# Seven products of quarters for the gate and up tiles, and issue in text order in the feed forward layers and the recurrence

## The chip, the core and the metric

The kernel runs on one core of a Trainium2 chip. Its engines are TensorE (PE in the profile, its weight loads PEld), VectorE (DVE), ScalarE (ACT), GpSimd (POOL) and SyncE (SP), which issues the DMAs. The metric is the device time of one execution in microseconds (us).

## The reference, cut to what matters

512 tokens of width 1024 go through two macaron layers (feed forward, mixer, feed forward; the mixer is stick-breaking attention in the first and a linear recurrence in the second) and then through two hybrid attention layers. All arrays are float32. The part that the change touches most is the feed forward layer, which occurs four times:

```
def sublayer_input(x, g, mod_j):
    shift, scale, gate = mod_j[:, 0], mod_j[:, 1], mod_j[:, 2]
    h = rmsnorm(x, g) * (1 + scale[:, None, :]) + shift[:, None, :]
    return h, (1 + gate)[:, None, :]

def swiglu(h, w_gu, w_down):                 # w_gu 1024 x 5632, w_down 2816 x 1024
    g, u = jnp.split(h @ w_gu, 2, axis=-1)
    return (jax.nn.silu(g) * u) @ w_down

mod = (silu(c) @ mod_w[layer] + mod_b[layer]).reshape(B, 3, 3, D_MODEL)
x = x + 0.5 * g * swiglu(h, ffn_w_gu[layer, 0], ffn_w_down[layer, 0])
```

The recurrence (`rglru_block`) projects h, convolves over four tokens, forms two sigmoid gates, runs a linear scan over the tokens, multiplies by gelu of a gate and projects back.

## The kernel before, in words

**Layout.** Everything is kept transposed: x, h and all projections are tiles of 128 features x 512 tokens. To reach float32 accuracy each operand is split into a rounded high part (fp32r, by a cast) and a low part (by a subtraction), and each product is three matmuls, high x high, high x low and low x high (`proj`). Matmuls accumulate in PSUM banks of 128 x 512; the tags are mm (four banks), z (two), T and o (one each).

**The weight stream.** All weights and modulation matrices are laid out on the host in the order of use (`segments`, `layout`) as entries of 128 x 1024. `stream_dma` loads entries into a ring of RAW = 4 buffers, `raw`. `stream_step` turns a weight entry into two chunks of 512 columns: the cast to `wh` on ScalarE, the subtraction to `wl` on VectorE, or on GpSimd for a share of them that `pool_low` sets (1.0 in `begin` and in the recurrence, 0 in the rest of the feed forward layers). A chunk holds four slots of 128 x 128, and `take` gives one slot to a row of matmuls, having run `stream_step` for AHEAD = 4 chunks in advance. A modulation entry is multiplied with silu(c) and summed on VectorE in one operation of 1024 columns (CUSTOM_DVE_ANT_0 in the profile) into one column of a modulation vector; the tuples at `mod(...)` in `segments` say between which fractions of a layer's entries the eight entries of each vector lie.

**A feed forward layer** (`ffn`) starts with the job "first": `begin` multiplies the weights of the first 4 columns (6 in the first layer) with x times the scale, before the norm's factor is known, while a chain (`factors`) sums the squares, takes the inverse root on VectorE, spreads it with TensorE and forms h in eight tiles `hH`, `hL`. The shift's share is added later by column sums `wshift` (`shift_cols`). Then 22 pairs f of a gate tile and an up tile follow, each tile 8 row blocks x 3 matmuls of 512 columns (jobs gu), with an evacuation `evac` on ScalarE and VectorE: silu, product, cast, low part. Last come 8 down tiles (jobs dn) of 22 x 3 matmuls each, after each of which x is updated, squared (GpSimd) and scaled for the next layer (`whole`).

**Order.** In the mixer attention and the hybrid layers a planner keeps one clock per engine (`clocked`) and a virtual time of TensorE, and all engines issue in the order of the program's text under `planned()`. In the feed forward layers and the recurrence the delays are fixed (`yield 0.7`) and, outside `begin`, the framework's own scheduler orders the instructions of an engine. In the recurrence (`lru`), `second` waits until all ten `om` tiles exist and then issues the ten scans (`beta`), after which the gelu outputs `ge` follow.

The planner's prices, in `clocked`, for n columns:

```
vector:  d = 0.15 + n / 960.0            clock advances by d - 0.082
         if not bank and n > 8: d += 0.58 * (overlap with GpSimd's operations)
scalar:  d = (0.162 if bank else 0.2) + n / 1210.0
gpsimd:  d = 0.12 + n / (440.0 if two else 900.0)      clock advances by d - 0.045
mm:      cost = max(0.112, 0.007 + n * 0.00043)
```

In the profile line L547 is the matmul in `mm`, L551 the transposition, L328 the helper that passes on every operation of VectorE, ScalarE and GpSimd.

## Time and profile before

| | |
|---|---|
| time, median of 3 runs | 3085.96 us (3082.9 to 3088.1) |
| the profiled execution | 3085.68 us, its span 3084.0 us |
| TensorE | 2977.1 us busy, 97%, 13752 matmuls |
| VectorE, ScalarE, GpSimd | 62%, 43%, 35% busy |
| DMA | 400.53 MB, mean 130 GB/s, 39.2% of the 16 engines |

The profile is one execution, with times from the start of its span. A matmul's recorded time overlaps that of its neighbours, so its price is the distance from one start to the next. A row of a group gives the busy time, the mean of one in ns, the idle time ahead of it on its engine, and what ended that.

### The profile page before, as it was taken

How to read it: one execution, taken by the hardware profiler on the slowest of the kernel's cores; microseconds unless marked ns; L12 is line 12 of the kernel's file. 1: busy time of each engine (PE TensorE's matmuls, PEld its weight loads, DVE VectorE, ACT ScalarE, POOL GpSimd, SP SyncE). 2: the span in 40 equal slices, each digit the busy share in tenths (PEclk: the TensorE clock that was granted, in tenths of full speed). 3: DMA queues.
4: the chain of work that ended last, by engine and by line, in shares of the span. 5: the costliest groups of instructions: out<-in, count | busy, mean ns of one | idle time of the engine just before them, and what ended most of it. 6: DMA issues, size and time to landing. Idle time of an engine off the chain costs nothing. (4 is left out here: it accounts for less than half of the span.)

```text
span 3084.0 us, 39072 instructions
## 1 busy us (share of the span) xinstructions
PE 2977.1 (97%) x13752; PEld 2475.4 (80%) x13752; DVE 1902.0 (62%) x3409; ACT 1312.9 (43%) x2520; POOL 1085.0 (35%) x802
## 2 busy tenths in 40 slices
PE   7999999989999999999899999999999999999998
PEld 5788877768888888887688888888888878888886
DVE  7844476676444655568965333578676556867653
ACT  3333245544332333324734333356456534645652
POOL 4554754440001200013531001343443684334466
PEclk9999999999999999999999999999999999999999
DMA  6454554413333344462222223354343335434322
GB/s 241 158 198 175 194 160 113 119 64 137 137 137 133 120 171 152 156 211 82 81 94 92 96 97 115 110 166 122 103 123 110 109 117 157 123 110 124 110 85 93
DMA packets 132643, 400.53 MB, mean 130 GB/s; under 512 B 18528, under 2 KB 19040, under 8 KB 132448
## 3 DMA queue, kind: packets, MB, share of 16 engines
q1 hardware_dynamic: 132448, 398.04, 39.2%
q8 instruction: 109, 1.79, 0.2%
q14 instruction: 86, 0.70, 0.1%
HBM read 343.44 MB, written 6.30 MB: 113 GB/s over the span
## 5 line engine op out<-in xcount | busy, mean ns | idle before, releaser
L328 POOL TENSOR_TENSOR wl<-raw,wh 128x512 fp32r<-128x512 f32 x574 | 815.3, 1427 | 905.1 <-ACT wh L328 852.2
L328 ACT CAST wh<-raw 128x512 fp32r<-128x512 f32 x968 | 596.0, 620 | 1063.3 <-PE mm L547 926.9
L547 PE MATMUL mm<-hH,wh 128*128 128x512 f32 x1584 | 622.1, 393 | 13.6 <-ACT ge L328 9.8
L547 PE MATMUL mm<-hL,wh 128*128 128x512 f32 x1584 | 620.6, 392 | 2.6 <-DVE hL L328 2.6
L547 PE MATMUL mm<-hH,wl 128*128 128x512 f32 x1584 | 619.7, 391 | 0.0
L328 DVE TENSOR_TENSOR wl<-raw,wh 128x512 fp32r<-128x512 f32 x396 | 290.3, 735 | 363.4 <-ACT wh L328 360.7
L547 PE MATMUL mm<-gH,wh 128*128 128x512 f32 x1016 | 407.2, 401 | 6.2 <-DVE v L328 3.9
L547 PE MATMUL mm<-gH,wl 128*128 128x512 f32 x1016 | 398.5, 392 | 1.5 <-POOL wl L328 1.5
L547 PE MATMUL mm<-gL,wh 128*128 128x512 f32 x1016 | 397.8, 392 | 0.0
L547 PEld LDWEIGHTS mm<-hH,wh 128*128 128x128 f32 x1584 | 299.6, 189 | 77.4 <-ACT ge L328 10.2
L547 PEld LDWEIGHTS mm<-hL,wh 128*128 128x128 f32 x1584 | 299.7, 189 | 67.0 <-DVE hL L328 5.3
L547 PEld LDWEIGHTS mm<-hH,wl 128*128 128x128 f32 x1584 | 299.5, 189 | 62.5
L328 DVE CUSTOM_DVE_ANT_0 raw<-raw,cact 128x1024 f32<-128x1024 f32 x144 | 207.8, 1446 | 187.0 <-DMA raw<-ws 180.1
L547 PE MATMUL mm<-aH,wl 128*128 128x512 f32 x704 | 274.0, 389 | 0.0
L547 PE MATMUL mm<-aH,wh 128*128 128x512 f32 x704 | 273.9, 389 | 0.0
L328 POOL TENSOR_TENSOR sq<-x 128x512 f32<-128x512 f32 x7 | 7.6, 1086 | 730.7 <-DVE x L328 730.7
L547 PEld LDWEIGHTS mm<-gH,wl 128*128 128x128 f32 x1016 | 191.4, 188 | 44.7 <-POOL wl L328 2.7
L547 PEld LDWEIGHTS mm<-gH,wh 128*128 128x128 f32 x1016 | 192.1, 189 | 42.0 <-issue 4.3
L547 PEld LDWEIGHTS mm<-gL,wh 128*128 128x128 f32 x1016 | 192.1, 189 | 35.0
L547 PEld LDWEIGHTS mm<-aH,wl 128*128 128x128 f32 x704 | 132.1, 188 | 27.6 <-POOL wl L328 0.4
L547 PEld LDWEIGHTS mm<-aH,wh 128*128 128x128 f32 x704 | 132.1, 188 | 27.5
L547 PE MATMUL mm<-wide,wh 128*128 128x512 f32 x384 | 149.4, 389 | 0.0
(271 smaller groups left out, 4706.6 us busy)
## 6 DMA issues: line engine op xcount, KB each, us to landing
raw<-ws SPq DMA_DIRECT2D x629, 512.0 KB, 3.3
ks<-rH SPq DMA_DIRECT2D x80, 128.0 KB, 3.2
kl<-rL SPq DMA_DIRECT2D x80, 128.0 KB, 2.6
qs<-rH SPq DMA_DIRECT2D x56, 128.0 KB, 3.9
qs<-rL SPq DMA_DIRECT2D x56, 128.0 KB, 3.7
keep<-ws SPq DMA_DIRECT2D x16, 256.0 KB, 5.9
ks<-qkH SPq DMA_DIRECT2D x32, 128.0 KB, 3.5
kl<-qkL SPq DMA_DIRECT2D x32, 128.0 KB, 3.1
```

What stands on the lines that cost most here:

```text
L328: r = f(*args, **kw)
L547: self.nc.tensor.matmul(out, lhsT, rhs, start=start, stop=stop, skip_group_check=True)
```

## The change

The gate and up tiles of 43 of the 88 pairs f are no longer computed as two tiles of eight row blocks, but as a 2 x 2 product of quarters in seven products (Strassen's scheme in Winograd's form): a, b are the gate's weights for the first and the second half of the 1024 features, c, d those of up, and the moving side is cut into two halves of 256 tokens. `SEVEN` names the pairs. Four sums of weights (s1 to s4) are formed by VectorE or GpSimd on the raw entries, then cast and split like other weights; `turned` forms the four sums of the moving side once per layer. Each product has 4 row blocks x 3 matmuls of 256 columns; the results are combined from PSUM by additions of 256 columns. The lookahead in these pairs is 6 chunks. The last product of a pair is run inside the next pair (`behind`).

Feed forward layers and the recurrence are issued in text order under the planner. Within it (`self.free`) each weight operand is a small process of its own (`operand`), and `either` chooses the engine of a subtraction or sum by the two clocks. Fixed delays become waits for the planner's clocks. The modulation entries move to the last part of each layer, six columns go into the first job of the second feed forward layer, and the shift sums of the first layer come 6 us later. The chunk tiles move from a pool of their own into the arena, which grows from 74 to 84 tiles.

The diff, cut to its core:

```diff
-FIRST = {(0, 0): 6, (0, 1): 4, (1, 0): 4, (1, 1): 4}
+FIRST = {(0, 0): 6, (0, 1): 6, (1, 0): 4, (1, 1): 4}
+SEVEN = {(0, 0): range(9, 17), (0, 1): range(6, 17), (1, 0): range(5, 17), (1, 1): range(5, 17)}
...
-        jobs += [(f"gu{j}", [gu[j]], KD) for j in range(n, 2 * KF)]
+        for f in range(n // 2, KF):
+            if f in SEVEN[l, i]:
+                jobs += [(f"q{f}", [gu[2 * f + u]], range(4 * part, 4 * part + 4)) for part in (0, 1) for u in (0, 1)]
+            else:
+                jobs += [(f"gu{j}", [gu[j]], KD) for j in (2 * f, 2 * f + 1)]
...
-    ffn(0, 0, [mod(0, 0, 2, 0.16, 0.28), mod(0, 1, 1, 0.28, 0.40), mod(0, 1, 0, 0.40, 0.52), mod(0, 1, 2, 0.52, 0.64),
-               mod(0, 2, 1, 0.68, 0.78), mod(0, 2, 0, 0.78, 0.88), mod(0, 2, 2, 0.88, 0.98)])
+    ffn(0, 0, [mod(0, 0, 2, 0.53, 0.60), mod(0, 1, 1, 0.60, 0.66), mod(0, 1, 0, 0.667, 0.73), mod(0, 1, 2, 0.73, 0.79),
+               mod(0, 2, 1, 0.79, 0.85), mod(0, 2, 0, 0.85, 0.91), mod(0, 2, 2, 0.91, 0.97)])
...
-    ffn(0, 1, [mod(1, 0, 1, 0.05, 0.35), mod(1, 0, 0, 0.35, 0.65), mod(1, 0, 2, 0.65, 0.95)])
-    ffn(1, 0, [mod(1, 1, 1, 0.02, 0.2), mod(1, 1, 0, 0.2, 0.4), mod(1, 1, 2, 0.4, 0.6),
-               mod(1, 2, 1, 0.68, 0.78), mod(1, 2, 0, 0.78, 0.88), mod(1, 2, 2, 0.88, 0.98)])
+    ffn(0, 1, [mod(1, 0, 1, 0.53, 0.65), mod(1, 0, 0, 0.667, 0.74), mod(1, 0, 2, 0.74, 0.81),
+               mod(1, 1, 1, 0.81, 0.88), mod(1, 1, 0, 0.88, 0.96)])
+    ffn(1, 0, [mod(1, 1, 2, 0.667, 0.74), mod(1, 2, 1, 0.74, 0.81), mod(1, 2, 0, 0.81, 0.88), mod(1, 2, 2, 0.88, 0.96)])
...
-    NSLOT = 74
+    NSLOT = 84
...
+    FAR = 6
...
+        if e[0] == "mod" and self.free:
+            self.spawn(self.product_sum(e[1], e[2], raw))
+            del self.raws[self.e_conv]
+            self.e_conv += 1
+            return
...
+        elif self.free and not self.w_half and type(raw) is not list:
+            self.operands(e, raw)
+            del self.raws[self.e_conv]
+            self.e_conv += 1
+            self.stream_dma()
...
+    def either(self, out, a, b, op):
+        if self.free:
+            t = max(self.made.get(x.tensor.name, 0.0) for x in (a, b))
+            pool = max(self.clock["gpsimd"], t) + 1.29 < max(self.clock["vector"], t) + 0.68 + 0.7
+        else:
+            self.pool_credit += self.pool_low
+            pool = self.pool_credit >= 1.0
+            if pool:
+                self.pool_credit -= 1.0
+        (self.nc.gpsimd if pool else self.nc.vector).tensor_tensor(out, a, b, op)
...
+    def operand(self, i, raws, first):
+        for r in self.reads.setdefault(i, raws):
+            yield max(0.01, self.made[r.tensor.name] - self.vt)
+        w = yield from first()
+        self.shifts(w, 4 * i)
+        h = self.t("wh", dt=F32R)
+        self.nc.scalar.copy(h, w)
+        yield
+        l = self.t("wl", dt=F32R)
+        self.either(l, w, h.bitcast(F32), OP.subtract)
+        self.parts[i] = (h, l)
+        del w, first
+        for r in raws:
+            self.left_raw[r.tensor.name] -= 1
+            if not self.left_raw[r.tensor.name]:
+                self.in_ring -= 1
+                self.stream_dma()
+        self.reads.pop(i)
+    def operands(self, e, raw):
+        def given(w):
+            yield 0.01
+            return w
+        def begin(raws, first):
+            self.w_conv += 1
+            self.spawn(self.operand(self.w_conv - 1, raws, first))
+        a, b = raw[:, 0:512], raw[:, 512:1024]
+        self.left_raw[raw.tensor.name] = 2
+        if e[0] == "w":
+            begin([raw], lambda: given(a))
+            begin([raw], lambda: given(b))
+        elif not self.quarter:
+            self.quarter = [raw, a, b]
+            begin([raw], lambda: given(a))
+        else:
+            last, a, c = self.quarter
+            self.quarter = None
+            b, d = raw[:, 0:512], raw[:, 512:1024]
+            self.left_raw[raw.tensor.name] = 3
+            sums = {}
+            def s1():
+                while 2 not in sums:
+                    yield 0.1
+                return sums[1]
+            def s2():
+                t = self.t("s1")
+                self.either(t, c, d, OP.add)
+                sums[1] = t
+                yield
+                t = self.t("s2")
+                self.either(t, sums[1], a, OP.subtract)
+                sums[2] = t
+                yield
+                return t
+            def s3():
+                t = self.t("s3")
+                self.either(t, a, c, OP.subtract)
+                yield
+                return t
+            def s4():
+                while 2 not in sums:
+                    yield 0.1
+                t = self.t("s4")
+                self.either(t, b, sums[2], OP.subtract)
+                yield
+                return t
+            begin([], s2)
+            if self.held:
+                old, rest = self.held
+                self.held = None
+                begin([old], lambda: given(rest))
+            begin([], s1)
+            begin([raw], lambda: given(b))
+            begin([last], s3)
+            begin([raw], s4)
+            if e[0] == "Q":
+                begin([raw], lambda: given(d))
+            else:
+                self.held = raw, d
...
+            yield 6.0
...
-            yield self.CHAIN[0] if (l, s) != (0, 2) else 7.0
+            if self.timed:
+                yield max(0.1, self.made[self.sq[0].tensor.name] - self.vt + 0.1)
+            else:
+                yield self.CHAIN[0]
             st = self.bank("o")
             self.colsum(st, 0, self.sq.pop(0), True)
             v = self.mean_eps(st[:, 0:4])
             self.rel("o")
-            d, bc = self.spread(self.rsqrt(v), "o")
-            yield self.CHAIN[1]
+            d = self.diagonal(self.rsqrt(v))
+            yield None if self.timed else self.CHAIN[1]
+            bc = yield from self.get("o")
             self.spread_mm(d, bc)
             self.inv = self.t("inv")
             nc.scalar.copy(self.inv, bc)
-            yield self.CHAIN[2]
+            yield None if self.timed else self.CHAIN[2]
             low = None
             for kt in range(KD):
                 nxt = self.h_high(kt, scale, shift, bc)
...
+    def turned(self, shift, tt):
+        nc = self.nc
+        ds = self.tiny("ds", 4)
+        nc.vector.tensor_tensor(ds, shift[:, 4:8], shift[:, 0:4], OP.subtract)
+        ht, self.ht = self.ht, []
+        for i in (0, 2):
+            t = [self.t(f"t{k}") for k in range(4)]
+            for j in (i, i + 1):
+                u, v = ht[j], ht[j + 4]
+                ab, cd = (u[:, 0:256], u[:, 256:512]), (v[:, 0:256], v[:, 256:512])
+                t1, t2, t3, t4 = (x[:, 256 * (j - i):256 * (j - i) + 256] for x in t)
+                s = shift[:, 4 + j:5 + j]
+                nc.vector.tensor_tensor(t1, ab[1], ab[0], OP.subtract)
+                yield 0.5
+                nc.vector.scalar_tensor_tensor(t2, cd[1], s, t1, OP.add, OP.subtract)
+                yield 0.5
+                nc.vector.scalar_tensor_tensor(t3, cd[1], ds[:, j:j + 1], ab[1], OP.add, OP.subtract)
+                yield 0.5
+                nc.vector.scalar_tensor_tensor(t4, cd[0], s, t2, OP.add, OP.subtract)
+                ht[j] = ht[j + 4] = None
+                yield 0.5
+            for k in (1, 0, 2, 3):
+                h, lo = self.t("tH", dt=F32R), self.t("tL", dt=F32R)
+                nc.scalar.copy(h, t[k])
+                yield
+                self.either(lo, t[k], h.bitcast(F32), OP.subtract)
+                t[k] = None
+                tt[k, i // 2] = h, lo
+                yield 0.8
+    def seven(self, f, tt, act, low, last):
+        nc = self.nc
+        def B(k, o):
+            return lambda i: tuple(x[:, o:o + 256] for x in self.h[i + k])
+        def T(k):
+            return lambda i: tuple(x[:, 256 * (i % 2):256 * (i % 2) + 256] for x in tt[k - 1, i // 2])
+        def product(bank, mov, first=True):
+            for i in range(4):
+                xh, xl = mov(i)
+                wh, wl = self.take(1)
+                for n, (w, x) in enumerate(((wh, xh), (wh, xl), (wl, xh))):
+                    self.mm(bank, w, x, first and i == n == 0, i == 3 and n == 2, again=i == n == 0)
+                self.pump()
+        for _ in range(4):
+            self.job(f"q{f}")
+        b1 = self.bank("mm")[:, 0:256]
+        product(b1, B(0, 0))
+        base = self.t("base", 256)
+        nc.scalar.copy(base, b1)
+        b2 = self.bank("z")[:, 0:256]
+        product(b2, T(2))
+        u2 = self.t("u2", 256)
+        nc.vector.tensor_tensor(u2, base, b2, OP.add)
+        self.rel("z")
+        if self.behind:
+            self.behind()
+        b3 = self.bank("z")[:, 0:256]
+        product(b3, T(1))
+        u4 = self.t("u4", 256)
+        nc.vector.tensor_tensor(u4, u2, b3, OP.add)
+        self.rel("z")
+        product(b1, B(4, 0), False)
+        g = self.t("sg")
+        nc.scalar.activation(g[:, 0:256], b1, AF.Silu)
+        self.rel("mm")
+        b7 = self.bank("mm")[:, 0:256]
+        product(b7, T(3))
+        up = self.t("a")
+        nc.vector.tensor_tensor(up[:, 256:512], u4, b7, OP.add)
+        b3 = self.bank("mm")[:, 0:256]
+        product(b3, B(4, 256))
+        nc.vector.tensor_tensor(u4, u4, b3, OP.add)
+        self.rel("mm")
+        def right():
+            yield
+            nc.scalar.activation(g[:, 256:512], u4, AF.Silu)
+        self.spawn(right(), 0.1)
+        def behind():
+            self.behind = None
+            product(b7, T(4), False)
+            nc.vector.tensor_tensor(up[:, 0:256], u2, b7, OP.add)
+            self.rel("mm")
+            self.spawn(rest())
+        def rest():
+            yield 0.1
+            yield
+            nc.vector.tensor_tensor(up, g, up, OP.mult)
+            yield
+            h = self.t("aH", dt=F32R)
+            nc.scalar.copy(h, up)
+            yield
+            lo = low[f] if f < 12 else self.t("aL", dt=F32R)
+            self.either(lo, up, h.bitcast(F32), OP.subtract)
+            act[f] = (h, lo)
+        if last:
+            behind()
+        else:
+            self.behind = behind
...
-        for j in range(n, 2 * KF):
-            ps, = self.proj(f"gu{j}", self.h_of)
-            if j % 2:
-                self.spawn(evac(j // 2, g, ps))
-            g = ps
+        with self.planned() if not self.timed else contextlib.nullcontext():
+            self.free = True
+            self.ffn_rest(l, i, n, act, low, evac)
+            self.free = False
+    def ffn_rest(self, l, i, n, act, low, evac):
+        nc = self.nc
+        s = 2 * i
+        tt = {}
+        turned = None
+        for f in range(n // 2, KF):
+            if f in SEVEN[l, i]:
+                self.need(lambda: turned.done)
+                self.look = self.FAR
+                self.seven(f, tt, act, low, f == SEVEN[l, i][-1])
+                if f == SEVEN[l, i][-1]:
+                    tt.clear()
+                    self.look = self.AHEAD
+                continue
+            for j in (2 * f, 2 * f + 1):
+                ps, = self.proj(f"gu{j}", self.h_of)
+                if turned is None and len(self.h) == KD:
+                    turned = self.spawn(self.turned(self.mods[l, s, 0], tt), 1.0)
+                if j % 2:
+                    self.spawn(evac(f, g, ps))
+                g = ps
...
-                self.ffn(l, i)
+                with self.planned() if l or i else contextlib.nullcontext():
+                    self.ffn(l, i)
...
-                    self.lru()
+                    with self.planned():
+                        self.lru()
+                        self.free = False
```

## Rows read from the trace of the kernel before

**Rows 1.** The page's part 1: busy us (share of the span) xinstructions.

```profile
PE 2977.1 (97%) x13752; PEld 2475.4 (80%) x13752; DVE 1902.0 (62%) x3409; ACT 1312.9 (43%) x2520; POOL 1085.0 (35%) x802
```

**Rows 2.** Windows, gate/up tiles: length; PE, PEld, DVE, ACT, POOL busy; clock, DMA share, GB/s.

```profile
120.00:225.00 105.00, 105.00 (x465) 86.95 (x464) 52.70 (x73) 36.19 (x64) 58.61 (x39) 1.00 0.57 199
740.00:925.00 185.00, 185.00 (x818) 153.19 (x817) 86.03 (x134) 61.30 (x102) 0.00 (x0) 1.00 0.40 137
1060.00:1255.00 195.00, 195.00 (x866) 161.57 (x865) 109.04 (x171) 69.22 (x116) 6.94 (x5) 1.00 0.45 159
1660.00:1855.00 195.00, 195.00 (x862) 161.48 (x861) 73.13 (x108) 64.61 (x108) 0.00 (x0) 1.00 0.28 97
```

**Rows 3.** Timeline of TensorE, second layer: start, recorded time, operation (14 rows left out).

```profile
799.75 0.39 PE L547 MATMUL mm<-hH,wl 128*128 128x512 f32 x1
...
803.14 0.39 PE L547 MATMUL mm<-hH,wl 128*128 128x512 f32 x1
```

**Rows 4.** Timeline of TensorE, first hybrid layer, 256 columns (18 rows left out).

```profile
2080.45 0.28 PE L547 MATMUL mm<-wl,gH 128*128 128x256 f32 x1
...
2082.73 0.28 PE L547 MATMUL mm<-wh,gL 128*128 128x256 f32 x1
```

**Rows 5.** Groups of VectorE by shape: busy us, mean ns, idle before.

```profile
L328 DVE CUSTOM_DVE_ANT_0 raw<-raw,cact 128x1024 f32<-128x1024 f32 x144 | 207.8, 1446 | 187.0 <-DMA raw<-ws 180.1 <-POOL wl L328 4.4 <-issue 2.4
L328 DVE TENSOR_TENSOR r<-r,sw 128x512 f32<-128x512 f32 x48 | 42.0, 874 | 0.3
L328 DVE TENSOR_TENSOR r<-mm,rope 128x512 f32<-128x512 f32 x48 | 32.3, 674 | 0.0
L328 DVE TENSOR_TENSOR wide<-T,wide 128x256 fp32r<-128x256 f32 x40 | 14.9, 413 | 0.7 <-PE mm L547 0.4 <-ACT wide L328 0.3
```

**Rows 6.** Groups of ScalarE by shape.

```profile
L328 ACT CAST wh<-raw 128x512 fp32r<-128x512 f32 x968 | 596.0, 620 | 1063.3 <-PE mm L547 926.9 <-issue 76.7 <-DMA raw<-ws 19.3
```

**Rows 7.** Timeline of VectorE and GpSimd in the second layer's down tiles.

```profile
957.47 1.35 POOL L328 TENSOR_TENSOR sqt<-x 128x512 f32<-128x512 f32 x1 [13.92 <-DVE x L328]
958.12 1.25 DVE L328 SCALAR_TENSOR_TENSOR gL<-x,mod,gH 128x512 fp32r<-128x512 f32 x1 [0.19 <-ACT gH L328]
958.90 1.62 POOL L328 TENSOR_TENSOR sq<-sq,sqt 128x512 f32<-128x512 f32 x1
959.76 1.31 DVE L328 TENSOR_TENSOR wl<-raw,wh 128x512 fp32r<-128x512 f32 x1 [0.39 <-ACT wh L328]
...
962.60 0.69 DVE L328 TENSOR_TENSOR wl<-raw,wh 128x512 fp32r<-128x512 f32 x1
```

**Rows 8.** Timelines of GpSimd and of VectorE in the recurrence.

```profile
1518.66 9.18 POOL L328 TENSOR_TENSOR wl<-raw,wh 128x512 fp32r<-128x512 f32 x5 [2.42 <-ACT wh L328]
...
1518.95 3.42 DVE L328 SCALAR_TENSOR_TENSOR ix<-ix,om 128x512 f32<-128x512 f32 x2
1522.29 4.48 DVE L328 TENSOR_TENSOR_SCAN om<-ra,ix 128x512 f32<-128x512 f32 x2
```

**Rows 9.** The page: DMA share and rate of 40 slices; loads of the stream.

```profile
DMA  6454554413333344462222223354343335434322
GB/s 241 158 198 175 194 160 113 119 64 137 137 137 133 120 171 152 156 211 82 81 94 92 96 97 115 110 166 122 103 123 110 109 117 157 123 110 124 110 85 93
...
raw<-ws SPq DMA_DIRECT2D x629, 512.0 KB, 3.3
```

**Rows 10.** Timeline of TensorE at its three pauses in changed code.

```profile
112.13 0.59 PE L547 MATMUL T<-ones,wshift 128*128 128x1 f32 x2 [5.32 <-DVE wshift L328]
...
113.15 0.63 PE L547 MATMUL mm<-hL,wh 128*128 128x512 f32 x1
113.58 0.63 PE L547 MATMUL mm<-hH,wl 128*128 128x512 f32 x1
...
688.16 1.08 PE L547 MATMUL o<-ones,sq 128*128 128x1 f32 x5 [4.76 <-DVE sq L328]
...
1535.85 0.80 PE L547 MATMUL mm<-hH,wh 128*128 128x512 f32 x1 [9.77 <-ACT ge L328]
```

More of the change, by code (lines that the diff above doesn't have):

```diff
@@ L189, in first_slots @@
                     slot += len(cols) // 128
+            if job[0] == "pad":
+                slot += job[2]
+            if job[0][0] == "q" and job[0][1:].isdigit():
+                slot += 3
     return out
@@ L202, in layout @@
         for job in jobs:
+            if job[0] == "pad":
+                slots += job[2] * [None]
+            if job[0][0] == "q" and job[0][1:].isdigit():
+                assert len(slots) % 4 == 0
+                quarters.add(len(slots) // 8)
             for kt in rows_of(job):
@@ L227, in layout @@
         if c >= n:
-            entries.append(("w", slots[8 * c:8 * c + 8]))
+            entries.append((("q" if c + 1 in quarters else "Q") if c in quarters else "w", slots[8 * c:8 * c + 8]))
         entries += at.get(c, [])
@@ L536, in room, with mm @@
         self.apart |= set(heads)
-    def mm(self, out, lhsT, rhs, start, stop, cost=None):
+    def mm(self, out, lhsT, rhs, start, stop, cost=None, again=False):
         if cost is None:
@@ L547, in mm @@
         self.nc.tensor.matmul(out, lhsT, rhs, start=start, stop=stop, skip_group_check=True)
-        self.matmul_at(out, (lhsT, rhs), cost, start)
+        self.matmul_at(out, (lhsT, rhs), cost, start or again)
     def transpose(self, out, in_):
@@ L570, in stream_init @@
         self.w_conv = 0
+        self.w_half = 0
+        self.quarter = self.held = None
+        self.reads, self.left_raw = {}, {}
+        self.free = False
         self.n_w, self.kept = 0, []
@@ L602, in stream_dma @@
                 break
+            for r in raw if type(raw) is list else (raw,):
+                self.made[r.tensor.name] = self.vt + 5.0
             self.raws[self.e_dma] = raw
@@ new lines, in two_parts, with product_sum @@
+    def two_parts(self, w):
+        h, l = self.t("wh", dt=F32R), self.t("wl", dt=F32R)
+        self.nc.scalar.copy(h, w)
+        self.either(l, w, h.bitcast(F32), OP.subtract)
+        self.parts[self.w_conv] = (h, l)
+        self.w_conv += 1
+    def product_sum(self, vec, m, raw):
+        if vec not in self.mods:
+            self.mods[vec] = self.modp.tile([128, 8], F32, name=self.name("mod"), tag="mod", bufs=12)
+        out = self.mods[vec]
+        yield max(0.01, self.made[raw.tensor.name] - self.vt)
+        self.nc.vector.tensor_tensor_reduce(raw, raw, self.cact, 1.0, 0.0, OP.mult, OP.add, accum_out=out[:, m:m + 1])
+        del raw
+        self.in_ring -= 1
+        self.stream_dma()
+        self.full.add((vec, m))
+        if all((vec, k) in self.full for k in range(KD)):
+            self.mod_end(vec, 0, KD)
+            self.full.add((vec, KD))
@@ L692, in take @@
         self.slot += n
+        if c not in self.parts:
+            self.need(lambda: c in self.parts)
         h, l = self.parts[c]
@@ L755, in mod_of @@
     def mod_of(self, vec):
-        assert (vec, KD - 1) in self.full, vec
+        self.need(lambda: all((vec, k) in self.full for k in range(KD)))
         return self.mods[vec]
@@ L1045, in evac @@
                 nc.scalar.activation(sg, g, AF.Silu)
-                yield 0.7
+                yield
                 nc.vector.tensor_tensor(a, sg, u, OP.mult)
@@ L1237, in parts @@
             else:
+                while self.inv is None:
+                    yield 0.3
                 t = self.t("qk")
@@ L1385, in conv @@
             if late is not None:
+                while self.inv is None:
+                    yield 0.3
                 t = self.t("xt")
@@ L1399, in conv @@
                 self.rel(tag)
-            yield 3.8
+            yield
             h = self.t("xH", dt=F32R)
             nc.scalar.copy(h, x)
-            yield 0.8
+            yield
             l = self.t("xL", dt=F32R)
@@ L1418, in gate_ri @@
             nc.scalar.activation(tu, tr, AF.Tanh, scale=self.sp4[:, c], bias=self.sp4[:, c])
-            yield 1.5
+            yield
             ix[n] = self.t("ix")
@@ L1423, in gate_ri @@
             nc.gpsimd.tensor_tensor(a2, a_[n], a_[n], OP.mult)
-            yield 2.5
+            yield
             o = self.t("om")
@@ L1461, in lru @@
         for name in [j[0] for j in self.jobs]:
+            if name == "pad":
+                self.parts.pop(self.slot // 4 - 1, None)
+                self.slot += self.job(name)[2]
+                continue
             n = int(name[2:])
             if name[:2] == "xb":
-                ps, = self.proj(name, self.hmov)
+                ps, = self.proj(name, self.h_of)
                 self.spawn(conv(n, ps))
```

90 lines of the change are left out of this document (41 added, 49 removed).

## The prediction, made before the kernel was run

> **What bounds the kernel now.** I read the page's busy times first. TensorE is busy 97% of the span, the other engines 35 to 62% [rows 1]. Then the windows over the gate and up tiles of the four feed forward layers: TensorE is busy through all of them at full granted clock, VectorE for 38 to 56%, ScalarE for about a third, and GpSimd not at all in two of the four [rows 2]. So here the time is the number of matmuls times their spacing. Third, that spacing. The busy time of one (0.39 us) overlaps its neighbours, so I take start to start: 15 steps in 3.39 us, 0.2267 us for 512 columns [rows 3], and 19 steps in 2.28 us, 0.120 us for 256 columns where each matmul also has its own weights [rows 4]. Half the columns cost 53% of the time.
>
> **The seven products.** A tile pair f (gate and up) now takes 2 x 8 x 3 = 48 matmuls of 512 columns: 48 x 0.2267 = 10.88 us. By the change it takes 7 x 4 x 3 = 84 of 256: 84 x 0.120 = 10.08 us. That is 0.80 us less on TensorE, and SEVEN names 8 + 11 + 12 + 12 = 43 of the 88 pairs: -34.4 us, if all else stays hidden.
>
> The Trainium skill, "TensorE: Matmul & The Clock Gate", section "Back-to-back issue gap", gives a warm gap of N / 2.4 + 2.5 ns, so 109 and 216 ns; as an estimate by it a pair would go from 10.36 to 9.17 us and 43 pairs would gain 51 us. The rows show about 11 ns more at either width, and the extra counts 84 times against 48; the measurement decides.
>
> What it adds beside TensorE, for each of the 43 pairs. Weight operands go from 4 chunks of 512 columns to 7 (an ACT cast and a subtraction each), and there are four new sums s1 to s4 of 512 columns. With the product's own low part, 12 operations of 512 columns go through `either`, to VectorE or GpSimd. Fixed on VectorE are the product g*up (512 columns, both inputs in SBUF) and five additions of 256 columns that read PSUM. ScalarE: 8 casts at 0.62 and three operations of half the width, at most 11 x 0.62 = 6.8 us in 10.08 [rows 6], covered.
>
> Which engine takes the 12: `either` picks GpSimd if its clock is no more than 0.09 us behind VectorE's (1.29 against 0.68 + 0.7), so it fills both equally, by the planner's prices: 1.24 us on GpSimd, 0.60 on VectorE plus 0.58 of the overlap with GpSimd (about 0.86 in all), 0.34 for each of the five additions. From 1.24 x = 5 x 0.34 + 0.60 + 0.86 (12 - x), x = 6.0. Six on GpSimd, and seven on VectorE with two SBUF inputs.
>
> The trace does not price this as the planner does. In [rows 7] VectorE's gL starts at 958.12 while GpSimd works until 958.82, and ends at 959.37, 0.55 us after it; GpSimd's sq, started meanwhile, ends at 960.52, 1.15 after gL; VectorE's wl, which takes about 0.69 alone (962.60 in the same rows), starts at 959.76 and ends at 961.07, 0.55 after sq. The two never work on such operands at once. [Rows 8] show the sum: five of GpSimd took 9.18 us beside two products and two scans of VectorE; 5 x 1.15 + 2 x 0.55 + 2 x 1.05 = 8.95. What reads PSUM is not held up: r<-mm,rope has a mean of 674 ns in the stage where r<-r,sw has 874 [rows 5]. In the gate and up stretches before, such work was little: four subtractions a pair, on VectorE alone in two of the four layers [rows 2].
>
> So a pair needs of this shared resource 6 x 1.15 + 7 x 0.55 = 10.75 us, more than TensorE's 10.08. That is the floor. The ceiling is that the five additions hide nothing: 6 x 1.70 + 0.69 + 5 x 0.41 = 12.95 (an addition from PSUM of 256 columns 0.41, a product alone 0.69 [rows 5]). [Rows 8] (97% of the resource used while both engines had work waiting) are near the floor, but VectorE issues in text order and s1, s2, cast and low part of the second product are one chain, so I count two of the five additions as not hidden: 10.75 + 0.82 = 11.6 us. Against 10.88 that is 43 x 0.72 = **+31 us** (floor -6, ceiling +89). The lookahead of six chunks doesn't help, since it delays a shortage and doesn't supply more.
>
> **Preparing the x side** (`turned`): per layer 16 operations of 256 columns and 8 casts with low parts, issued while two or more plain pairs run: 16 x 0.41 + 8 x 0.69 = 12 us of VectorE inside at least 2 x 10.88, beside their own ten operations. Zero; if it overran, 5 us a layer.
>
> **The modulation columns move** to the end of each layer. Each is one entry of the stream on VectorE (1.45 us [rows 5]). In the first layer 56 now lie in 0.53 to 0.97 of 66 weight entries: 29 + 56 entries of 0.524 MB in 29 x 5.44 = 158 us, 282 GB/s; in the third 51 entries in 105 us, 256 GB/s. The highest slice before has 241 GB/s, at a DMA share of 0.6 [rows 9], and a landing takes 3.3 us with four buffers. I take zero because that share leaves room; if 241 were the limit it would cost 27 + 7 = 34 us. VectorE's 81 us lie in 158 us.
>
> **Issue in text order, and the waits at the seams.** Three pauses of TensorE lie in code that changes [rows 10]. At 107 us it waits 5.3 us for wshift, and the next ten matmuls go at 0.43 us start to start (about half speed): 7.3 us. The added `yield 6.0` puts these small matmuls behind 6 us of other work: -7 (0 if wshift comes later still). At 683 us it waits 4.8 us for sq, then eleven slow matmuls: 7.0 us. The first job of that layer now has six columns, not four, and the chain's start comes from the modelled end of sq: -7 (0 if the model is early again). At 1526 us it waits 9.8 us for a bank that ScalarE's ge frees, itself behind the scans on VectorE and the contention of [rows 8]; with the order of `second()` unchanged I give -5, between -15 and +10. Together **-19 us** (-29 to +10).
>
> **Sum.** 3085.7 (the profiled execution; its span is 3084.0, and the median of the runs is 3086.0, so nothing is corrected) + 31 - 19 = **3098 us**.
>
> **Rivals.** (a) The cover holds and TensorE sets the pace: faster. For it: TensorE was never idle in these stretches, VectorE has 44% or more left, and `either` may use GpSimd less than I count. It decides at five on GpSimd: 5 x 1.15 + 8 x 0.55 = 10.15 us, level with 10.08. Against it: the planner's equal filling gives six. Time: 3085.7 - 34.4 - 19 = 3032.
> (b) The additions hide nothing and chains wait for each other: 12.95 us a pair, 3085.7 + 89 - 19 = 3156; pauses of some 2 us per pair could also lower the clock, as after some of the pauses before. For it: text order on all engines means one late subtraction holds the whole queue. Against: the 97% of [rows 8].
> (c) The stream at the ends of the layers is limited at 241 GB/s while the rest is as forecast: 3098 + 34 = 3132. For it: no slice before moved more. Against: the DMA share of 0.6.
>
> **How the numbers follow.** Forecast (the shared operands bind, at 10.9 to 12.2 us a pair) 0.55: 3085.7 + 1 - 19 = 3068 to 3085.7 + 57 - 19 = 3124, with the spread of the seams 3060 to 3135. Of it I put 0.08 on faster and 0.09 on no change (at 11.3 us a pair the surcharge of 19 us and the seams cancel), 0.38 on slower. (a) 0.27, faster. (b) 0.12 and (c) 0.06, slower. Runs of this kernel differ by 0.2%, about 6 us, and a smaller change can't be told from none. Faster: 0.27 + 0.08 = 0.35; same: 0.09; slower: 0.38 + 0.12 + 0.06 = 0.56. The range reaches down to (a), and up past (c) and into (b): 3032 to 3145.
>
> **What would show it.** Right: in the gate and up stretches TensorE's busy share falls to about 0.87, with idle time ahead of products 2 to 6 released by GpSimd's or VectorE's wl; about six operations a pair on GpSimd; their mean near 1.6 us and VectorE's of two SBUF inputs over 1.2; 84 matmuls at 0.120 us where they run without a pause. (a) would show TensorE without a gap in these stretches, a pair every 10.1 us. (c) would show TensorE waiting for casts that wait for raw in the first and third layers' down tiles. The seams: no pause over 2 us at 107 and 683. The prediction is wrong if a pair takes under 10.5 us or GpSimd takes four or fewer of the twelve.

## The result, and the profile after

The changed kernel takes 3200.77 us (median of 4 runs, 3197.49 to 3204.15); the kernel before, beside it, 3087.03. The ratio is 1.0365 [1.0341, 1.039]: slower by 114 us, where the forecast was 12 us slower and the range ended at 3145. The profiled execution has a span of 3195.7 us, 111.7 more than before. The ratios of the experiments are to the kernel before, run beside each group of them (its medians there 3090.6 to 3094.6 us), so kernels of different groups are compared by ratio.

The page's busy times, which answer to [rows 1]:

```profile
PE 3000.5 (94%) x15304; PEld 2560.0 (80%) x15304; DVE 2354.6 (74%) x3656; ACT 1368.5 (43%) x2763; POOL 1697.5 (53%) x1183
```

VectorE and GpSimd have gained 453 and 613 us of busy time for 247 and 381 more instructions: it is not only more work, each piece is longer. Windows over the pairs of seven products and, last, over the first layer's down tiles (as [rows 2]; length, busy times of PE, PEld, DVE, ACT, POOL, clock, DMA share, GB/s):

```profile
160.00:245.00 85.00, 75.94 (x587) 74.72 (x587) 73.27 (x82) 36.37 (x73) 65.92 (x41) 0.94 0.27 91
800.00:920.00 120.00, 101.78 (x784) 99.54 (x783) 108.04 (x116) 51.62 (x105) 95.72 (x58) 0.94 0.28 89
1175.00:1305.00 130.00, 115.46 (x862) 113.57 (x863) 117.63 (x125) 57.23 (x115) 103.92 (x63) 0.91 0.27 86
1760.00:1890.00 130.00, 112.49 (x867) 110.26 (x866) 118.45 (x127) 57.13 (x115) 105.03 (x63) 0.95 0.27 88
299.00:427.00 128.00, 122.03 (x530) 98.55 (x529) 98.57 (x115) 30.02 (x52) 66.53 (x43) 1.00 0.68 237
```

TensorE was busy all the time in these stretches before; now it is for 85 to 89%, and VectorE for 86 to 91%. The groups of GpSimd (first fence) and of VectorE (second) from 1180 to 1300 us, in the third layer:

```profile
L346 POOL TENSOR_TENSOR wl<-raw,wh 128x512 fp32r<-128x512 f32 x19 | 31.9, 1678 | 19.7 <-ACT wh L346 17.5 <-issue 2.2
L346 POOL TENSOR_TENSOR wl<-s,wh 128x512 fp32r<-128x512 f32 x11 | 18.4, 1680 | 0.0
L346 POOL TENSOR_TENSOR s<-raw 128x512 f32<-128x512 f32 x10 | 17.4, 1742 | 0.0
L346 POOL TENSOR_TENSOR s<-raw,s 128x512 f32<-128x512 f32 x10 | 17.3, 1730 | 0.1
L346 POOL TENSOR_TENSOR wide<-a,aH 128x512 fp32r<-128x512 f32 x7 | 12.1, 1733 | 0.0
L346 POOL TENSOR_TENSOR aL<-a,aH 128x512 fp32r<-128x512 f32 x2 | 3.5, 1728 | 0.0
L346 POOL TENSOR_TENSOR s<-s,raw 128x512 f32<-128x512 f32 x1 | 1.7, 1741 | 0.0
```

```profile
L346 DVE TENSOR_TENSOR wl<-s,wh 128x512 fp32r<-128x512 f32 x29 | 44.7, 1542 | 1.8 <-ACT wh L346 1.8
L346 DVE TENSOR_TENSOR wl<-raw,wh 128x512 fp32r<-128x512 f32 x11 | 18.2, 1655 | 0.3
L346 DVE TENSOR_TENSOR a<-sg,a 128x512 f32<-128x512 f32 x10 | 17.8, 1779 | 0.0
L346 DVE TENSOR_TENSOR s<-s,raw 128x512 f32<-128x512 f32 x9 | 13.0, 1447 | 0.0
L346 DVE TENSOR_TENSOR a<-u,mm 128x256 f32<-128x256 f32 x20 | 8.2, 408 | 0.1
```

A pair takes 12.1 to 12.3 us here (start to start of the SiLU of its first half), so these 120 us hold 9.8 pairs: the 60 operations of GpSimd are six a pair, as the prediction counted, at 1.7 us each. The product `a<-sg,a`, 0.69 us alone, takes 1.78; the addition that reads PSUM still 0.41. The timelines show why, GpSimd's first, then VectorE's:

```profile
1207.83 1.74 POOL L346 TENSOR_TENSOR s<-raw,s 128x512 f32<-128x512 f32 x1
1209.53 1.74 POOL L346 TENSOR_TENSOR wl<-s,wh 128x512 fp32r<-128x512 f32 x1
```

```profile
1206.63 1.78 DVE L346 TENSOR_TENSOR a<-sg,a 128x512 f32<-128x512 f32 x1
1208.33 1.78 DVE L346 TENSOR_TENSOR wl<-s,wh 128x512 fp32r<-128x512 f32 x1
1210.04 0.41 DVE L346 TENSOR_TENSOR u<-u,z 128x256 f32<-128x256 f32 x1
```

VectorE's wl ends at 1210.11, 0.54 after GpSimd's sum (1209.57); GpSimd's next ends at 1211.27, 1.16 after that. It is the alternation of [rows 7], now all the way. TensorE pays once a pair, in the second or third product (timeline of TensorE):

```profile
1197.22 0.28 PE L568 MATMUL z<-tH,wh 128*128 128x256 f32 x1
1197.34 0.28 PE L568 MATMUL z<-tL,wh 128*128 128x256 f32 x1
1199.57 0.39 PE L568 MATMUL z<-tH,wl 128*128 128x256 f32 x1 [1.94 <-DVE wl L346]
1199.79 0.28 PE L568 MATMUL z<-tH,wh 128*128 128x256 f32 x1
1199.91 0.28 PE L568 MATMUL z<-tL,wh 128*128 128x256 f32 x1
1200.03 0.28 PE L568 MATMUL z<-tH,wl 128*128 128x256 f32 x1
```

Without a pause a step is 0.12 us, as taken from [rows 4]. Soon behind the pause shown TensorE does some 16 steps at 0.21 us: the granted clock from 1200.5 to 1203.6 is 0.50, the lower of its two levels, and 1.00 again from 1204 to 1211. From 1180 to 1300 us TensorE waits 11.1 us for VectorE's wl, in eight waits, and some 70 slow steps take about 7 us more than at full clock. As it still waits in most pairs, I read the slow steps as filling time in which it would have waited; no run separates the two.

Stages, from TensorE's first and last matmul of the down tiles (and of the mixers' output tiles) in each profiled execution, in us; the kernels beyond the first two are experiments below:

| | before | after | eight, shared (no_quarters) | vec_pad |
|---|---|---|---|---|
| gate/up, four layers | 284.9 + 250.9 + 242.8 + 243.6 = 1022.2 | 299.4 + 276.0 + 265.1 + 267.0 = 1107.5 | 283.4 + 259.2 + 243.5 + 246.2 = 1032.3 | 276.5 + 253.3 + 238.0 + 240.6 = 1008.4 |
| first down tiles | 119.7 | 127.7 | 133.3 | 119.5 |
| attention | 270.9 | 278.5 | 274.5 | 272.7 |
| recurrence | 206.4 | 198.6 | 200.2 | 198.3 |
| hybrid layers and end | 1106.3 | 1124.1 | 1122.5 | 1109.6 |

### The profile page after: what moved, and what is told of

It is laid out like the page before. It is cut to its first block, busy times and chain, and to the rows that moved or that the text cites. A ratio compares the mean times of both kernels' runs of the same rounds, so it can differ in the third digit from the quotient of the medians.

```text
span 3195.7 us, 43280 instructions
## 1 busy us (share of the span) xinstructions
PE 3000.5 (94%) x15304; PEld 2560.0 (80%) x15304; DVE 2354.6 (74%) x3656; ACT 1368.5 (43%) x2763; POOL 1697.5 (53%) x1183
## 4 chain that ended last, share of the span: by engine, by line
PE 47%; DVE 22%; issue 4%; ACT 2%; POOL 2%; DMA 1%; SPq 0%; DVEq 0%; POOLq 0%; ACTq 0%
PE mm L568 39%; DVE wl L346 5%; PE z L568 4%; DVE a L346 2%; PE o L568 2%; DVE s L346 1%; PE T L572 1%; DVE t L346 1%; POOL wl L346 1%; DVE hL L346 1%; DVE xc L346 1%; DVE sw L346 1%; DMA raw<-ws 1%; DVE wide L346 1%; DVE u L346 1%
## 5 line engine op out<-in xcount | busy, mean ns | idle before, releaser
L346 POOL TENSOR_TENSOR wl<-raw,wh 128x512 fp32r<-128x512 f32 x741 | 1090.7, 1482 | 1164.3 <-ACT wh L346 1005.0
L346 ACT CAST wh<-raw 128x512 fp32r<-128x512 f32 x927 | 535.6, 617 | 263.8 <-DMA raw<-ws 239.9
L568 PE MATMUL mm<-hH,wh 128*128 128x512 f32 (+1 forms) x1396 | 495.9, 355 | 10.0 <-ACT base L346 5.3
L568 PE MATMUL mm<-hL,wh 128*128 128x512 f32 (+1 forms) x1396 | 494.0, 354 | 4.9 <-DVE hL L346 4.8
L568 PE MATMUL mm<-hH,wl 128*128 128x512 f32 (+1 forms) x1396 | 493.2, 353 | 1.0 <-POOL wl L346 1.0
L568 PEld LDWEIGHTS mm<-hL,wh 128*128 128x128 f32 x1396 | 267.2, 191 | 43.1 <-DVE hL L346 9.5
L568 PEld LDWEIGHTS mm<-hH,wl 128*128 128x128 f32 x1396 | 267.0, 191 | 36.4 <-POOL wl L346 1.5
L568 PE MATMUL mm<-aH,wh 128*128 128x512 f32 x704 | 274.5, 390 | 3.9 <-ACT wh L346 3.9
L346 DVE CUSTOM_DVE_ANT_0 raw<-raw,cact 128x1024 f32<-128x1024 f32 x144 | 241.0, 1699 | 18.6 <-DMA raw<-ws 12.3
L346 DVE TENSOR_TENSOR wl<-s,wh 128x512 fp32r<-128x512 f32 x116 | 180.0, 1554 | 8.9 <-ACT wh L346 8.7
L568 PE MATMUL z<-tH,wl 128*128 128x256 f32 x344 | 107.8, 313 | 62.2 <-DVE wl L346 42.1
```

The source lines that it names most:

```text
L346: r = f(*args, **kw)
L568: self.nc.tensor.matmul(out, lhsT, rhs, start=start, stop=stop, skip_group_check=True)
```

## The experiments

Three theories after the result. **S**: the sharing with GpSimd is what makes a pair 12.3 us. **M**: the modulation entries, crowded into the ends of the layers, cost the first down tiles. **H**: the hybrid layers (+17.8), whose TensorE and VectorE text is the same in both kernels, suffer from the `pad`: the change puts four empty slots, half an entry, behind the weights of the recurrence, which shifts every later entry of the stream by half an entry (a part of the diff that isn't shown above). The rivals are named in the expectations.

**vec_only**: `either` always takes VectorE within `ffn_rest`.

```
-            pool = max(self.clock["gpsimd"], t) + 1.29 < max(self.clock["vector"], t) + 0.68 + 0.7
+            pool = not self.vec_only and max(self.clock["gpsimd"], t) + 1.29 < ...
...
-            self.free = True
+            self.free = self.vec_only = True
             self.ffn_rest(l, i, n, act, low, evac)
```

> After with one edit: in the gate, up pairs of the feed forward layers `either` always takes VectorE. Theory S (VectorE and GpSimd exclude each other on operands in SBUF): VectorE needs 13 x 0.60 + 5 x 0.34 = 9.5 us a pair and nothing holds it up, so a pair falls from 12.3 us to 10.1 to 10.5 and the time from 3201 by about 43 x 1.9 = 80 us to 3110 to 3125. Rival Q (the chain sum, sum, cast, subtraction and the text order set the pair, whatever the engine): thirteen operations in one queue are no faster than six and seven in two, the pair stays at 12 us or above, 3190 or more.

Measured: 3079.57 us, ratio to before 0.9954 [0.9939, 0.9969], 121 us under the changed kernel (127 by the ratios), and below the 3110 of the expectation. S holds, and more hung on it than I had put there: the ends of the runs and the first down tiles came back too. The same windows of this kernel, with the same seven products:

```profile
160.00:215.00 55.00, 53.54 (x444) 53.13 (x443) 51.02 (x96) 28.29 (x60) 0.00 (x0) 1.00 0.30 106
770.00:860.00 90.00, 88.30 (x730) 87.54 (x730) 83.11 (x158) 45.92 (x96) 0.00 (x0) 1.00 0.31 106
1120.00:1215.00 95.00, 92.28 (x761) 91.29 (x760) 87.43 (x165) 49.90 (x103) 0.00 (x0) 1.00 0.31 106
1670.00:1770.00 100.00, 98.30 (x813) 97.53 (x813) 93.17 (x175) 52.25 (x106) 0.00 (x0) 1.00 0.30 107
275.00:394.00 119.00, 119.00 (x527) 98.54 (x526) 93.43 (x147) 29.61 (x51) 16.66 (x13) 1.00 0.78 264
```

TensorE is back at 97 to 98%, the clock at full, with all 18 operations of a pair on one engine that is 92 to 93% busy: two engines together did less than VectorE alone. The last row is the first layer's down tiles: TensorE never waits while the stream moves 264 GB/s, above the 241 of [rows 9].

**no_quarters**: eight products everywhere, the rest of the change kept, GpSimd shared.

```
-                if turned is None and len(self.h) == KD:
+                if SEVEN[l, i] and turned is None and len(self.h) == KD:
...
-SEVEN = {(0, 0): range(9, 17), (0, 1): range(6, 17), (1, 0): range(5, 17), (1, 1): range(5, 17)}
+SEVEN = {(0, 0): (), (0, 1): (), (1, 0): (), (1, 1): ()}
```

> After with SEVEN empty (and no sums of the moving side): all pairs by 48 matmuls of 512 columns, all else as in after. Theory S: the seven products cost about 70 to 85 us in all, so 3115 to 3130, and the gate and up stretches are as long as before (243 us in the third and fourth layer). Rival T (issue in text order under the planner slows the feed forward layers themselves): the gate and up stretches stay 10 us or more above before, 3150 or more.

Measured: 3120.49 us, 1.0089 [1.0074, 1.0104]. So about 80 of the 114 us are the quarters with their sharing (75 in the table's stages). What stays shows in the table: the second layer's gate and up stage, 8 us above before (the sq pause, below), the first down tiles, the hybrid layers.

**pad_back**: the pad is used up behind the last down tiles, not at the end of the stream.

```
     ffn(1, 1, [])
+    segs[-1][1].append(("pad", [], 4))
```

> After with a second pad of four empty slots behind the last feed forward layer, so that in the hybrid layers the weight entries begin at the same jobs as before the change. The hybrid layers took 1106 us before and 1124 after. Theory H (the pad ahead of the last feed forward layer shifted the entries by half an entry, and loads meet the stacking DMAs at another moment): hybrid layers back to 1106 to 1112, 3183 to 3190 in all. Rival (the planner's modelled landing of raw, or the chunk tiles in the arena): hybrid layers stay at 1120 or more, 3197 or more.

Measured: 3184.34 us, 1.0288 [1.0271, 1.0305], 16 us less (24 by the ratios); the hybrid layers go from 1124.1 to 1110.4, 13.7 less, the surer measure. H holds for the shift as the cause. Windows over the hybrid layers: before, after, pad_back.

```profile
1977.70:3084.00 1106.30, 1074.06 (x5302) 910.00 (x5300) 743.27 (x1766) 562.54 (x1239) 538.57 (x405) 0.99 0.39 118
```

```profile
2071.70:3195.70 1124.00, 1082.94 (x5302) 915.90 (x5300) 755.51 (x1766) 548.17 (x1238) 527.78 (x404) 0.99 0.40 116
```

```profile
2073.20:3183.70 1110.50, 1077.71 (x5302) 911.87 (x5300) 759.19 (x1766) 549.03 (x1240) 531.39 (x406) 0.99 0.41 117
```

Equal work, and 17.8 us more after the change. Part of the way back is seen in TensorE's waits there, after and pad_back, for `kl`, which a DMA copies from `rL`:

```profile
PE z L568 <- DMA kl<-rL: 7.4, 4, 2.1
```

```profile
PE z L569 <- DMA kl<-rL: 2.7, 2, 1.4
```

That is 4.7 of the 13.7 us. But the kernel before had 4.9 us of this wait, so between before and after it explains only 2.5 of 17.8; the rest is spread over waits that I haven't taken apart, and by what mechanism the shift costs time isn't shown.

**plain_mods**: no_quarters with the modulation entries where they were before.

```
-    ffn(0, 0, [mod(0, 0, 2, 0.53, 0.60), mod(0, 1, 1, 0.60, 0.66), ...
+    ffn(0, 0, [mod(0, 0, 2, 0.16, 0.28), mod(0, 1, 1, 0.28, 0.40), ...
```

> no_quarters with the modulation entries of the first three feed forward layers where they were before. The first layer's down tiles took 119.7 us before and 127.7 after. Theory M (56 modulation entries in the last 0.44 of the layer ask for more than the stream delivers): back to 119.7, so 6 to 10 us under no_quarters. Rival (GpSimd and VectorE exclude each other there as well): stays at 125 or more, no_quarters within 3 us.

Measured: 3109.93 us, 1.0054 [1.0039, 1.0069], 10.6 us less, with the first down tiles back from 133.3 to 119.5. So the moved entries do cost, but not by a limit of the DMAs: vec_only has them in the same place at 264 GB/s without a pause, and eight_vec below runs these tiles in 119.6. It takes both, the crowding and the engines that hold each other up: neither plain_mods (sharing alone) nor eight_vec (crowding alone) loses anything there. In the changed kernel ScalarE's casts wait for loads there (waits, 299 to 427 us: engine, line, waited for, us in total, times, longest):

```profile
ACT wh L346 <- DMA raw<-ws: 75.3, 17, 9.4
POOL wl L346 <- ACT wh L346: 52.2, 17, 6.4
```

These waits alone would have looked like a slow DMA.

**vec_pad**: vec_only and pad_back together.

> Both repairs together: in the feed forward layers every operation that `either` chooses goes to VectorE, and the half entry of the weight stream (the pad) is used up at the end of the last feed forward layer, as before the change, rather than at the end of the stream. Theory H (the pad's shift costs the hybrid layers 10 to 18 us whatever the feed forward layers do): 3079.6 - 10 to 14 = 3066 to 3070, hybrid layers from 1120 back to 1106 to 1111 us, the gate and up stages as in vec_only. Rival (the pad only mattered where GpSimd was already late at the end of the feed forward layers): no gain, 3078 to 3081, hybrid layers at 1118 to 1120.

Measured: 3069.4 us, 0.9923 [0.9909, 0.9938]; hybrid layers 1109.6 for vec_only's 1120.1. H also without the sharing.

**sq_late**: vec_pad with a later issue of the sums of sq at the seam to the second layer.

```
-                yield max(0.1, self.made[self.sq[0].tensor.name] - self.vt + 0.1)
+                yield max(0.1, ... + 0.1) + (10.0 if (l, s) == (0, 2) else 0.0)
```

> vec_pad, and in the second feed forward layer the column sums of sq are issued 10 us later by the planner's clock (some 40 matmuls of the first job lie ahead of them instead of 6). Theory P (the 9 us pause at 670 us is only a wrong place in the text: the planner takes sq as ready before it is): the pause disappears and so do the slow matmuls behind it, 8 to 12 us off vec_pad, about 3057 to 3061. Rival (the x tiles that the next matmuls read come out of the same late chain as sq): the pause moves to the next column of tiles, 0 to 2 us off. Second rival (the normalisation that follows is on the path): the pause comes back 10 us later in front of the first gate or up tile that needs the normalised x, no gain.

Measured: 3063.17 us, 0.9907 [0.989, 0.9924], 6 us less: between theory and first rival. The pause in the changed kernel (vec_pad's has the same 8.97), and what sq_late has in its place:

```profile
717.95 1.84 PE L568 MATMUL o<-ones,sq 128*128 128x1 f32 x8 [8.97 <-DVE sq L346]
719.65 0.77 PE L568 MATMUL mm<-gH,wh 128*128 128x512 f32 x1
720.22 0.63 PE L568 MATMUL mm<-gL,wh 128*128 128x512 f32 x1
```

```profile
675.34 0.77 PE L569 MATMUL mm<-gH,wh 128*128 128x512 f32 x1 [4.15 <-DVE x L347]
677.98 0.80 PE L569 MATMUL mm<-gH,wh 128*128 128x512 f32 x1 [1.01 <-DVE x L347]
688.84 0.95 PE L569 MATMUL o<-ones,sq 128*128 128x1 f32 x8
```

Of 9 us, 5 remain as waits of an x tile: 4 us were the place in the text, 5 the late chain. The kernel before paid 4.8 us at this seam too.

**pool_one and pool_three**: on vec_pad, a fixed one or three of the twelve operations of a pair on GpSimd.

```
-                self.either(t, c, d, OP.add)
+                self.either(t, c, d, OP.add, True)       # s1: both kernels
...
+                self.either(t, a, c, OP.subtract, True)  # s3: pool_three
...
+            self.either(lo, up, h.bitcast(F32), OP.subtract, True)  # pool_three
```

> vec_pad with one of the twelve operations of a pair on GpSimd: the sum s1, whose operands are raw weights and come early. Theory E (GpSimd and VectorE exclude each other on operands from SBUF: one operation on GpSimd holds VectorE for 1.15 us and saves it 0.64): a pair goes from 10.3 to between 10.5 and 10.8 us, 43 x 0.2 to 0.5 = 9 to 22 us more than vec_pad. Rival (the exclusion falls beside the five additions that read PSUM, so one operation is free and takes 0.64 us from VectorE, which at 92% busy is now what limits): a pair at 10.08 us, TensorE's own time, 5 to 10 us less than vec_pad.

> vec_pad with three of the twelve operations of a pair on GpSimd: s1, s3 and the low part of the product. Theory E: six on GpSimd made a pair 12.3 us against 10.3 with none, 0.33 us each, so three make 11.0 to 11.3 and 43 x 0.7 to 1.0 = 30 to 43 us more than vec_pad. Rival (a threshold, as in the prediction's sum: up to five on GpSimd the shared operands fit under TensorE's 10.08 us): 3 x 1.15 + 10 x 0.55 = 8.95 us fit, so a pair stays at 10.1 to 10.3 and the time is within 5 us of vec_pad or below it.

Measured: 3066.24 us, 0.9915 [0.99, 0.993], and 3071.89 us, 0.9933 [0.9919, 0.9948], against vec_pad's 0.9923. My theory E, a price for each operation, fell: up to three cost nothing. They gain nothing clear of the intervals either; pool_one's rival had 5 to 10 us. That left two explanations of six: their number, or which ones the planner takes.

**pool_four and pool_six**: the low part of the raw quarter b as fourth; those of a and d as fifth and sixth.

```
-            begin([raw], lambda: given(b))
+            begin([raw], lambda: given(b), True)   # its low part goes to GpSimd
```

> vec_pad with four of the twelve operations of a pair on GpSimd: s1, s3, the low part of the product, and the low part of the raw quarter b. Pairs so far: 10.3 us with none or one on GpSimd, 10.27 with three, 12.3 with the six that the planner chose. Theory N (the number decides: the shared operands cost 1.15 us for each on GpSimd and 0.55 for each on VectorE, and 1.6 of the 2.05 us of the additions from PSUM are not hidden, 8.75 + 0.6 g; below 10.1 to 10.3 it is covered): 11.1 us, or 10.9 by the 0.3 that this formula gave too much at three; 43 x 0.6 to 0.85 = 25 to 37 us over vec_pad's 3069, 3094 to 3106. Rival W (which operations decide: the planner's six include low parts of sums, links of the chains s1, s2, cast, low part, and these make TensorE wait): raw quarters come early, so nothing is late, within 6 us of vec_pad, 3063 to 3075.

> vec_pad with six of the twelve operations of a pair on GpSimd, as many as the planner put there, but others: s1, s3, the low part of the product, and the low parts of the three raw quarters a, b and d. Theory N: 8.75 + 0.6 x 6 = 12.3 us a pair as in the changed kernel, 43 x 2.0 = 86 us over vec_pad, with the ends of the runs 3150 to 3165. Rival W (raw quarters come early and hold no chain): a pair below 11.2, under 40 us over vec_pad, below 3110.

Measured: 3092.36 us, 1.001 [1.0, 1.0019], and 3154.89 us, 1.0204 [1.0189, 1.0219]. Theory N holds for six: with raw quarters, which hold no chain, they cost as much as the planner's six, and rival W falls. With four the pair is a little under N's 10.9 to 11.1. The mean period of the eight steady pairs of the third layer, by the number on GpSimd:

| on GpSimd | 0 | 1 | 3 | 4 | 6 | 6, the planner's |
|---|---|---|---|---|---|---|
| us a pair | 10.35 | 10.25 | 10.34 | 10.80 | 12.40 | 12.23 |

The kernels with three, four and six in the same layer:

```profile
1120.00:1215.00 95.00, 95.00 (x781) 93.97 (x781) 82.35 (x142) 49.13 (x101) 41.72 (x28) 1.00 0.35 107
```

```profile
1130.00:1225.00 95.00, 91.42 (x745) 89.59 (x744) 82.37 (x125) 47.71 (x99) 52.64 (x36) 1.00 0.29 97
```

```profile
1170.00:1290.00 120.00, 105.64 (x784) 103.27 (x785) 100.60 (x117) 50.88 (x105) 81.94 (x52) 0.93 0.30 96
```

With three, TensorE has no gap; with four it has small ones; with six, pairs alternate between 9.6 and some 15.2 us and the granted clock falls. It is a knee, between three and four. The formula 8.75 + 0.6 g, whose 1.6 us came from a kernel with six, gives 10.55, 11.15 and 12.35 for three, four and six: right at six, 0.2 to 0.35 too much below, so it places the knee only roughly.

**eight_vec**: vec_pad with eight products everywhere.

> vec_pad with eight products in every pair (no quarters), all else the same: what the seven products are worth once nothing stands in their way. Theory: a plain pair is 10.88 us, a pair of seven products 10.3 (VectorE at 92% busy, TensorE's own 10.08), so 43 x 0.58 = 25 us over vec_pad, 3094. First rival (the term of the prediction in full, 43 x 0.80): 34 us, 3103. Second rival (nearly all of vec_pad's gain over the kernel before is from text order and the places of the entries, not from the products): within 8 us of vec_pad, 3070 to 3077.

Measured: 3091.95 us, 1.0002 [0.9992, 1.0012], against vec_pad's 0.9923: the seven products are worth 0.8%, about 23 us, once they aren't shared away. 43 x (10.88 - 10.35) = 23; the gate and up stages of the two profiles, 1026.9 and 1008.4, differ by 18.5. Against the kernel before, eight_vec is level: the rest of the change, with the sharing away and the pad moved, gains nothing on the whole, and the second rival falls.

**late_one**: sq_late and s1 on GpSimd.

> The two edits that gave something, together on vec_pad: the column sums 10 us later (6.2 us less) and s1 alone on GpSimd (3.2 us less). If they lie in different stretches and add: 3060. If the 3.2 us were the noise of one program's layout rather than s1: as sq_late, 3063, or above.

Measured: 3063.48 us, 0.9912 [0.9897, 0.9926], the same as sq_late: the 3 us of pool_one don't add, and lie within the intervals. sq_late stands as the fastest, some 29 us under the kernel before.

## Why the prediction was wrong, point by point

**Counts and spacings: right.** 84 matmuls at 0.120 us, six operations a pair on GpSimd, seven of two inputs on VectorE, 0.55 and 1.15 us after each other's end. All the signs that the prediction named as right came, but for the seams', and the time still lay outside its range: the mechanism was right, and sizes were wrong.

**The price of a pair: the step that failed first.** "I count two of the five additions as not hidden: 10.75 + 0.82 = 11.6 us." It is 12.3: by its sum 1.55 of the additions' 2.05 us show, not 0.82, nearer to the ceiling (12.95) than to the floor. [Rows 8] misled me: there the sharers had work waiting all along. Here GpSimd waits for ScalarE's cast in nearly every pair (17.5 us before the `wl<-raw,wh` of its groups above). In one such wait, on GpSimd's, VectorE's and ScalarE's timelines:

```profile
1202.84 1.61 POOL L346 TENSOR_TENSOR wl<-raw,wh 128x512 fp32r<-128x512 f32 x1 [2.19 <-ACT wh L346]
```

```profile
1199.77 1.44 DVE L346 TENSOR_TENSOR wl<-s,wh 128x512 fp32r<-128x512 f32 x1
1201.13 0.41 DVE L346 TENSOR_TENSOR u<-u,mm 128x256 f32<-128x256 f32 x1
1202.28 0.42 DVE L346 TENSOR_TENSOR u<-base,z 128x256 f32<-128x256 f32 x1 [0.74 <-ACT base L346]
1202.62 0.69 DVE L346 TENSOR_TENSOR s<-raw,raw 128x512 f32<-128x512 f32 x1
```

```profile
1201.57 0.42 ACT L346 ACTIVATE sg<-u 128x256 f32<-128x256 f32 x1 [3.63 <-DVE u L346]
1202.14 1.66 ACT L346 CAST wh<-raw 128x512 fp32r<-128x512 f32 x3
```

From 1201.21, where VectorE's wl ends, to 1202.62 neither engine works on the shared operands: VectorE does two additions and waits itself. These 1.4 us and the floor of 10.75 make 12.15 of the 12.3. The chain behind the gap isn't the one that the prediction named: VectorE's addition `u<-u,mm` comes behind the wl shown, ScalarE's SiLU of the second half waits 3.6 us for it, and the cast that GpSimd needs stands behind this SiLU in ScalarE's text order. Whether the cast ahead of the SiLU would close the gap, no run tests.

43 x 0.7 is 30 us. The last pair of each run of such pairs takes 14.7 to 15.8 us, for which the cause isn't shown: another 12 in all, not in the sum. From the first to the last matmul of the quarters the 43 pairs take 541 us, 12.6 each (446 in vec_pad), which is 73 us above 43 x 10.88. In the table, the quarters cost 1107.5 - 1032.3 = 75 us where I had +31; the ceiling of +89 held. The x side (`turned`) cost nothing visible, as forecast: up to the first matmul of the quarters the third layer takes 58.6 us with the sharing and without.

**The seams in the gate and up stages: wrong sign.** Forecast -14, measured 1032.3 - 1022.2 = +10. At the first layer the wait for wshift did shrink, from 5.3 us to 1.1 and 2.5; without the sharing (eight_vec) that stage is 277.9, the forecast 7 us below before, and with it 283.4 (no_quarters). The second layer's is 259 in both, 8 above before instead of 7 below, as the sq pause grew from 4.76 [rows 10] to 8.97: "the chain's start comes from the modelled end of sq" was the danger that the prediction named ("0 if the model is early again"), and it had priced it at zero rather than at a loss. The planner puts the sums behind nine matmuls of the job; the fixed 7 us had put them behind 33.

**The recurrence: right**, -7.8 for -5: the wait of 9.8 us for ge is gone, against 3.4 us of new waits for `tr` and 1.6 more for `xL`.

**What the sum left out.** The zero for the moved modulation columns holds for the DMAs, so rival (c) is refuted as a mechanism. But the entries' subtractions and sums met the shared operands in the first down tiles: +8. The hybrid layers, +17.8, I took as untouched because their code is; the pad moved every entry of their stream by a half. Attention gained 7.6 us, of which 1.8 are left in vec_pad; its other variants range to 6.1, and I haven't settled where that lies.

**The whole.** 75 + 10 - 8 + 8 + 8 + 18 is 111 of 111.7 us, the last 1 in the later down tiles. The sum had 31 - 14 - 5. Rival (b)'s 3156 came nearest, by too high a price of a pair; its chains that wait for each other and its lower clock (0.91 to 0.95 in the windows above) are there. The ends of the runs, the sq pause and the stages that I had left out made up for the price and more.

## What to carry to other kernels

Two engines that exclude each other on the same kind of operand are one engine with two queues: give the second one only what the first can't fit under the bound, and look for the knee (here between three and four operations of twelve) rather than for equal filling. A stage whose instructions are unchanged still depends on how the stream ahead of it is cut; half an entry was worth 10 to 14 us. When a planner orders the text, an operation that it thinks ready too early can cost more than the fixed delay that it replaces: here the pause grew from 4.8 to 9.0 us.

## What the runs showed of the hardware that was not expected

The alternation is very regular: in the changed kernel some 390 operations of VectorE on 512 columns and two SBUF inputs saw one end of GpSimd's, and ended 548 ns after it (546 to 552 for the middle 80%); GpSimd ended 1.15 us after VectorE's (1.13 to 1.16). Together a pair of operations takes 1.70 us where VectorE alone does two in 1.37, so handing one over loses time as soon as both have work waiting. And the core took 264 GB/s over 119 us at a DMA share of 0.78 with no stall of TensorE.
